# GLA levels on the columns of second block halves, and no meta columns after the last layer's mixing

## The chip, the cores and the metric

One core of a Trainium2 chip runs the whole program. The metric is the device time of one execution in microseconds. Before the change it is 2452.31 us (median of 3 runs, 2452.1 to 2452.59).

## The reference

One inference step of a decoder trunk with two layers, in float32. The columns (tokens) are 512 prompt tokens behind 16 learned meta tokens, and 8 samples of 4 tokens with a past of 512. Each layer is:

```
x += 0.5 * SwiGLU_1(RMSNorm(x))                      # 1024 -> 2 x 2816 -> 1024
h  = RMSNorm(x); columns of h @ W_in for three head groups
x += W_out [ FoX(h) | SSD(h) | GLA(h) ]              # forgetting attention, Mamba-2, gated linear attention
x += 0.5 * SwiGLU_2(RMSNorm(x))
```

The GLA group (4 heads, key 32, value 64) works in blocks of 128 tokens (16 for the meta tokens, 4 for a sample). With bc the running sum of the log gates of a block:

```
att = einsum('bthk,bshk,btshk->btsh', qc, kc, exp(bc_t - bc_s))     # s <= t
o   = att @ vc + (qc * exp(bc)) @ state
```

The result is y of the prompt without the meta tokens (`xp[:, N_META:]`), y of the samples, and the new keys, values, log forget values and states of both layers.

## The kernel before

x lies transposed in SBUF, 8 tiles of 128 rows by 560 columns: 32 of the samples, 16 meta columns, 512 of the prompt. Two groups of columns go through everything: A (columns 0 to 303: samples, meta, two blocks of the prompt; tiles 4, 0 and 1) and B (304 to 559: two blocks, tiles 2 and 3). Tile 4 holds the 48 columns of samples and meta tokens.

Every large product is made of three matmuls (`mm3`, line 427): weights and inputs are split into a high and a low part (`whi`, `wlo`, `hhi`, `hlo`, `hid`), and high x high, high x low and low x high are summed in PSUM. The weights come by DMA into `raw`, ScalarE casts the high part, VectorE (in the mixing stage each fifth time GpSimd) subtracts the low one.

A channel mixing (`ffn`) goes through 22 units of the hidden width, each with a gate and an up unit of weights: 24 matmuls on A, 24 on B. The down projection is done in three parts of 8, 8 and 6 units, in each for 8 tiles of rows. In the last part group A comes first, then B (`ffn_out`, the weights kept), so that A's norm runs beside B's matmuls. `norm` sums squares on ScalarE and GpSimd, turns the factor into rows on TensorE, and makes `hhi` and `hlo`.

The mixing stage (`mix`) names its pieces in `MIX_ORDER` (line 160); a scheduler of the framework then interleaves their instructions, engine by engine, so that the order on an engine is not that of the code. Each of the three head groups has a piece per tile: `fox_tile` (and `fox_meta` for the meta rows of tile 4, `fox_decode` for the samples), `ssd_tile`, `gla_tile`. They write into O; `split_o`, `mix_out` and `norm` follow.

`gla_tile` makes att by levels. For m = 64, 32, 16, 8, 4 a block of 2m columns has an early and a late half; key columns of the early half act on query columns of the late one. The first two levels of a tile of 128 columns are already made on the late halves alone (`z0`, `z1`, 256 columns for four heads). The others, m = 16, 8, 4 (in tile 4 the levels 8 and 4), are made on all columns: `zq` (lines 1221 and 1222; the third on GpSimd, being in `ON_POOL`) is the query times the gates for four heads, 512 columns, one fp32 matmul with the keys (line 1224) gives 128 x 512 values, and a masked copy (line 1225) puts those into `att` that the mask `lev` admits:

```
zq = self.g2(4 * n)
self.tt(zq..., z.unsqueeze(1).to_broadcast([128, 4, n]), qm, eng=self.e(f"gzq{i}"))
self.mm(pa[:n, :4 * n], kk, zq)
V.copy_predicated(out=att, mask=masks["lev"][:, i, :]..., data=pa[:n, :4 * n]...)
```

What is within a distance of three comes from `band` (line 1243). Tiles 4, 0, 1 of GLA come early in the stage, gla:2 and gla:3 late, beside SSD and FoX tiles and group A's output projection.

Of the kernel before, what the change touches and what calls it, by code (L numbers as in the profile page):

```python
# [25 lines left out]
F32R = mybir.dt.float32r  # L26
# [8 lines left out]
L = 2  # L35
D = 1024
# [50 lines left out]
def constants():  # L87
# [50 lines left out]
    for m in LEVS:  # L138
        s_, t_ = P[:, None], P[None, :]
        lev.append((s_ // (2 * m) == t_ // (2 * m)) & ((s_ // m) % 2 == 0) & ((t_ // m) % 2 == 1))  # L140
    put("lev", np.stack(lev[2:], 1))
    put("lev4", np.stack([v[:48, :48] & same for v in lev[3:]], 1))
    band = [k + d == t for d in (1, 2, 3)]
# [46 lines left out]
for _n, _w in (("gb", 128), ("fb", 4), ("db", 8), ("al", 8), ("sd", 8)):  # L190
# [37 lines left out]
class Trunk:  # L228
    def __init__(self, tc, a, es):
        self.tc, self.a = tc, a  # L230
        self.nc = nc = tc.nc
        self.V, self.S, self.G, self.T = nc.vector, nc.scalar, nc.gpsimd, nc.tensor
        pool = lambda n, b, **k: es.enter_context(tc.tile_pool(name=n, bufs=b, **k))
        self.pers = pool("pers", 1)
        self.wp = pool("wp", 2)
        self.hp = pool("hp", 1)
        self.tmp = pool("tmp", 1)
        self.psg = pool("psg", 2, space=PSUM)
        self.uid = 0
# [233 lines left out]
    def norm(self, g, gain, order=range(8)):  # L473
        c0, n = GRP[g]
        x = self.x
        acc = None
        for i, k in enumerate(order):
            sq = self.s1(304)
            self.act(sq[:, :n], x[:, k, c0:c0 + n], AF.Square)
            if i == 0:  # L480
                acc = sq
            else:
                self.tt(acc[:, :n], acc[:, :n], sq[:, :n], ALU.add, self.G if i < 7 else self.V)
        tiles = TILES[g]
# [8 lines left out]
        hi = self.t([128, 8, n], "hhi" + g, dt=F32R, pool=self.hp)  # L493
        lo = self.t([128, 8, n], "hlo" + g, dt=F32R, pool=self.hp)
        for k in range(8):
            h = self.s1(304)
            self.stt(h[:, :n], x[:, k, c0:c0 + n], gain[:, k:k + 1], y, ALU.mult, ALU.mult)
            self.act(hi[:, k, :], h[:, :n])
            eng = NORM_LO["mix" + g if self.lo_pool else g][k]
            self.tt(lo[:, k, :], h[:, :n], hi[:, k, :].bitcast(F32), ALU.subtract, self.G if eng == "G" else self.V)  # L500
        return hi, lo

    def ffn_in(self, l, i, fs, groups, H, hid, kept=None):

        for f in fs:
            pss = {}
            for gu in range(2) if kept is None or groups == "A" else (1, 0):
                w = self.kept_unit(kept, (f, gu), self.a["win"][l, i, f, gu], (f, gu) == (FIRST - 1, 1))
                for g in groups:
                    n = GRP[g][1]  # L510
                    ps = pss[gu, g] = self.ps(self.psg if g == "A" and (kept is None or f % 2 == 0) else self.psx)
                    hi, lo = H[g]
                    self.mm3(ps[:, :n], [(w[k], (hi[:, k, :], lo[:, k, :])) for k in range(8)])
            for g in groups:
                n = GRP[g][1]
                pg, pu = pss[0, g][:, :n], pss[1, g][:, :n]
# [64 lines left out]
    def hid_alloc(self, f, g):  # L581
        n = GRP[g][1]
        return tuple(self.t([128, n], "hid" + g, F32R, 16, self.hid) for _ in range(2))
# [250 lines left out]
    def fox_tile(self, g, i, c0):  # L834
# [6 lines left out]
        for hp in range(2):  # L841
# [32 lines left out]
            for k in range(i + 2):  # L874
                for h2, (et, emt) in enumerate(ets):
# [4 lines left out]
                    else:  # L880
                        self.mm(o, self.Vm[:, d], emt, start=False, stop=True)
        self.act(self.O[g][:, 0:2, c0:c0 + 128], po[:, 0:256].rearrange("p (a b) -> p a b", a=2))

# [117 lines left out]
    def ssd_tile(self, l, g, j, ti, c0, n):  # L1001
# [136 lines left out]
        for f in range(4):  # L1138
            self.tr(pt[:, f * n:(f + 1) * n], y[:, 128 * f:128 * f + 128])
        self.tt(self.O[g][:, 2:6, cs], pt[:, :4 * n].rearrange("p (f t) -> p f t", f=4), self.col["sn"].unsqueeze(2).to_broadcast([128, 4, n]))  # L1140


    def gla_tile(self, l, g, j, ti, c0, n):
# [31 lines left out]
        for h in range(4):  # L1175
            self.act(att[:, h, :], self.c("ident")[:n, :n], scale=dd[:, h:h + 1])
        masks = {m: self.c(m + ("4_r" if last else "_r")).rearrange("p (m t) -> p m t", t=n) for m in ("lev", "band")}

# [33 lines left out]
        for i in range(2 if last else 3):  # L1212
# [101 lines left out]
        for hp in range(2):  # L1314
            self.tr(pt[:, hp * n:(hp + 1) * n], on[:, 128 * hp:128 * hp + 128])
        for hp in range(2):
            self.stt(self.O[g][:, 6 + hp, cs], pt[:, hp * n:(hp + 1) * n], self.col["gn"], R[f"gg{hp}"][:, cs], ALU.mult, ALU.mult)

    def split_o(self, g):
        n = GRP[g][1]  # L1320
        hi = self.t([128, 8, n], "hhi" + g, F32R, pool=self.hp)
        lo = self.t([128, 8, n], "hlo" + g, F32R, pool=self.hp)
        for k in range(8):
# [5 lines left out]
    def mix_out(self, l, g, O):  # L1329
        c0, n = GRP[g]  # L1330
        hi, lo = O
# [9 lines left out]
    def mix(self, l, H):  # L1341
# [3 lines left out]
        nc.sync.dma_start(out=self.sconv.rearrange("p f b i -> p (f b i)"), in_=self.a["sconv"][l])  # L1345
        self.cvout = self.t([128, 6, 9, 3], "cvout")
        self.R = {"A": {}, "B": {}}
        self.O, S, N = {}, {}, {}
        run, live = {}, {}
        for g in GRP:  # L1350
            for j, (ti, c0, n) in enumerate(TILES[g]):
                run["gla", ti] = lambda a=(l, g, j, ti, c0, n): self.gla_tile(*a)
                run["ssd", ti] = lambda a=(l, g, j, ti, c0, n): self.ssd_tile(*a)
                run["fox", ti] = (lambda a=(g, ti, c0): self.fox_tile(*a)) if ti < 4 else self.fox_meta
            run["gla_in", g] = lambda g=g: self.gla_in(l, g, H)
# [105 lines left out]
def gather(r):  # L1461
# [24 lines left out]
```

## Time and profile before

| | |
|---|---|
| median of the runs | 2452.31 us |
| the profiled execution | 2455.32 us, its span 2453.5 us |
| TensorE | 2368.8 us busy (97%), granted clock 0.986 |
| VectorE | 1256.3 us (51%) |
| ScalarE | 869.7 us (35%) |
| GpSimd | 523.7 us (21%) |
| DMA engines | 230.57 MB, q1 29.9% |

The page cuts the span into 40 slices. In the channel mixings TensorE is busy in nine tenths of a slice or more and VectorE in three to four; in the two mixing stages (slices 9 to 14 and 29 to 34, counted from 1) VectorE is at seven to nine and the granted clock falls below full in some slices. A busy time is a sum over such different stages, so what a change is worth has to be read stage by stage.

### The profile page before, as it was taken

What the parts mean: (1) busy time and instruction counts of PE and PEld (TensorE: products, weight loads), DVE (VectorE), ACT (ScalarE), POOL (GpSimd) and SP (SyncE); (2) the same over time, 40 slices, a digit from 0 to 9 for tenths busy, and PEclk for the clock granted to TensorE, in tenths of its full rate; (3) what the DMA queues carried; (4) which work ended last, traced back from release to release, by engine and by line L of the source; (5) the groups of instructions that cost most, each with busy time, mean ns of one, the idle gap of its engine ahead of it and who ended that gap; (6) DMA issues with size and microseconds to landing.
All of it is one profiled execution on the core that took longest, in us unless ns stands there. A gap on an engine that the chain in (4) does not pass through costs nothing. (4 is left out here: it accounts for less than half of the span.)

```text
span 2453.5 us, 44862 instructions
## 1 busy us (share of the span) xinstructions
PE 2368.8 (97%) x17908; PEld 2254.9 (92%) x17908; DVE 1256.3 (51%) x2675; ACT 869.7 (35%) x1902; POOL 523.7 (21%) x688
## 2 busy tenths in 40 slices
PE   8999999999889999999999999999998999999999
PEld 8999999987777899999999999999776779999999
DVE  5434345388788533333443333343888985333333
ACT  4323223444354432322333232334343544323231
POOL 3202124233232310100221010131423324101010
PEclk9999999989899999999999999999899999999999
DMA  4222223344322322222222222232443222222222
GB/s 150 88 87 87 87 86 96 95 123 135 116 79 66 106 85 86 87 87 86 87 78 86 86 85 83 87 101 86 129 135 102 88 90 87 87 86 87 87 84 84
DMA packets 89683, 230.57 MB, mean 94 GB/s; under 512 B 12706, under 2 KB 38050, under 8 KB 89474
## 3 DMA queue, kind: packets, MB, share of 16 engines
q1 hardware_dynamic: 89042, 227.54, 29.9%
q8 instruction: 141, 2.31, 0.4%
q14 instruction: 68, 0.56, 0.1%
q10 hardware_dynamic: 432, 0.16, 0.0%
HBM read 219.73 MB, written 7.92 MB: 93 GB/s over the span
## 5 line engine op out<-in xcount | busy, mean ns | idle before, releaser
L272 DVE TENSOR_TENSOR wlo<-raw,whi 128x512 fp32r<-128x512 f32 (+1 forms) x649 | 464.1, 718 | 404.5 <-ACT whi L278 395.1
L278 ACT ACTIVATE whi<-raw 128x512 fp32r<-128x512 f32 (+1 forms) x680 | 427.0, 631 | 646.0 <-PE ps L265 589.3
L265 PE MATMUL ps<-hhiA,wlo 128*128 128x304 f32 x1664 | 507.5, 305 | 0.0
L265 PE MATMUL ps<-hhiA,whi 128*128 128x304 f32 x1664 | 506.8, 305 | 0.0
L265 PE MATMUL ps<-hloA,whi 128*128 128x304 f32 x1664 | 505.6, 304 | 0.0
L265 PE MATMUL ps<-hhiB,wlo 128*128 128x256 f32 x1664 | 471.2, 283 | 4.4 <-POOL wlo L272 3.0
L265 PE MATMUL ps<-hhiB,whi 128*128 128x256 f32 x1664 | 469.6, 283 | 2.0 <-ACT s L278 0.9
L265 PE MATMUL ps<-hloB,whi 128*128 128x256 f32 x1664 | 469.5, 282 | 0.0
L265 PEld LDWEIGHTS ps<-hhiB,whi 128*128 128x128 f32 x1664 | 315.0, 189 | 6.1 <-issue 1.9
L265 PEld LDWEIGHTS ps<-hhiB,wlo 128*128 128x128 f32 x1664 | 315.2, 190 | 5.6 <-POOL wlo L272 3.2
L265 PEld LDWEIGHTS ps<-hhiA,wlo 128*128 128x128 f32 x1664 | 314.8, 189 | 3.9 <-issue 3.0
L265 PEld LDWEIGHTS ps<-hloA,whi 128*128 128x128 f32 x1664 | 315.3, 189 | 2.8 <-issue 2.0
L265 PEld LDWEIGHTS ps<-hhiA,whi 128*128 128x128 f32 x1664 | 314.7, 189 | 2.6 <-issue 1.4
L265 PEld LDWEIGHTS ps<-hloB,whi 128*128 128x128 f32 x1664 | 314.5, 189 | 2.3 <-issue 1.5
L272 POOL TENSOR_TENSOR hidA<-s,hidA 128x304 fp32r<-128x304 f32 x88 | 76.0, 864 | 849.2 <-ACT hidA L278 849.1
L265 PE MATMUL ps<-hidA,whi 128*128 128x304 f32 x1072 | 226.2, 302 | 0.0
L275 DVE SCALAR_TENSOR_TENSOR x<-ps,x 128x304 f32<-128x304 f32 (+1 forms) x192 | 86.0, 449 | 232.3 <-PE ps L265 230.7
L265 PE MATMUL ps<-hidB,whi 128*128 128x256 f32 x1072 | 193.9, 281 | 0.0
L265 PEld LDWEIGHTS ps<-hidA,whi 128*128 128x128 f32 x1072 | 174.4, 188 | 0.0
L265 PEld LDWEIGHTS ps<-hidB,whi 128*128 128x128 f32 x1072 | 166.2, 189 | 0.0
L272 DVE TENSOR_TENSOR s<-s,ps 128x256 f32<-128x256 f32 (+3 forms) x194 | 90.4, 467 | 145.7 <-PE ps L265 137.6
L265 PE MATMUL ps<-hidA,wlo 128*128 128x304 f32 x536 | 162.1, 302 | 0.0
(334 smaller groups left out, 3579.9 us busy)
## 6 DMA issues: line engine op xcount, KB each, us to landing
raw<-win SPq DMA_DIRECT2D x176, 512.0 KB, 3.5
raw<-wout SPq DMA_DIRECT2D x64, 512.0 KB, 3.5
raw<-wfm SPq DMA_DIRECT2D x48, 512.0 KB, 3.5
raw<-wmo SPq DMA_DIRECT2D x32, 512.0 KB, 3.6
raw<-wout SPq DMA_DIRECT2D x32, 384.0 KB, 3.5
pg<-kpage SPq DMA_DIRECT2D x64, 130.0 KB, 2.2
pg<-vpage SPq DMA_DIRECT2D x64, 128.0 KB, 2.3
raw<-wtm SPq DMA_DIRECT2D x8, 544.0 KB
```

Source lines behind the costliest of these rows:

```text
L265: return self.T.matmul(out, lhsT, rhs, start=start, stop=stop, **k)
L272: return (eng or self.V).tensor_tensor(out=out, in0=a, in1=b, op=op)
L275: return self.V.scalar_tensor_tensor(out=out, in0=a, scalar=s, in1=b, op0=op0, op1=op1)
L278: return self.S.activation(out, in_, f, **k)
```

## The change

In `gla_tile` the levels m = 16, 8, 4 are made on the late halves alone: `zq` has 2n columns in place of 4n, the matmul streams 2n, and the masked copy reads 2n and writes the late halves of `att`. The masks keep only those columns. In the last layer, from the output projection on, group A has 288 columns: at the head of its mixing stage the 32 sample columns of x are copied 16 columns up, over the meta columns, and `GRP_END`, `TILES_END` take the place of `GRP`, `TILES`; the tiles write into O without the meta columns, `fox_meta` is not called there, and the samples are read from y at 16 to 47.

```diff
-    put("lev", np.stack(lev[2:], 1))
-    put("lev4", np.stack([v[:48, :48] & same for v in lev[3:]], 1))
+    odd = lambda v, m: v[:, (np.arange(v.shape[1]) // m) % 2 == 1]
+    put("lev", np.stack([odd(v, m) for v, m in zip(lev[2:], LEVS[2:])], 1))
+    put("lev4", np.stack([odd(v[:48, :48] & same, m) for v, m in zip(lev[3:], LEVS[3:])], 1))
...
+GRP_END = {"A": (16, 288), "B": GRP["B"]}
+TILES_END = {"A": [(4, 0, 32), (0, 32, 128), (1, 160, 128)], "B": TILES["B"]}
...
     def norm(self, g, gain, order=range(8)):
-        c0, n = GRP[g]
+        c0, n = self.grp[g]
...
-        self.act(self.O[g][:, 0:2, c0:c0 + 128], po[:, 0:256].rearrange("p (a b) -> p a b", a=2))
+        self.act(self.O[g][:, 0:2, self.ocols(g, c0, 128)[0]], po[:, 0:256].rearrange("p (a b) -> p a b", a=2))
...
-            zq = self.g2(4 * n)
-            self.tt(zq.rearrange("p (h t) -> p h t", h=4), z.unsqueeze(1).to_broadcast([128, 4, n]), qm, eng=self.e(f"gzq{i}"))
+            m = LEVS[(3 if last else 2) + i]
+            half = lambda a: a.rearrange("p (b i m) -> p b i m", i=2, m=m)[:, :, 1, :]
+            zq = self.g2(2 * n)
+            zv = zq.rearrange("p (h b m) -> p h b m", h=4, m=m)
+            qv = qm.rearrange("p h (b i m) -> p h b i m", i=2, m=m)[:, :, :, 1, :]
+            self.tt(zv, half(z).unsqueeze(1).to_broadcast(list(qv.shape)), qv, eng=self.e(f"gzq{i}"))
             pa = self.ps(self.psL)
-            self.mm(pa[:n, :4 * n], kk, zq)
-            V.copy_predicated(out=att, mask=masks["lev"][:, i, :].unsqueeze(1).to_broadcast([n, 4, n]),
-                              data=pa[:n, :4 * n].rearrange("p (h t) -> p h t", h=4))
+            self.mm(pa[:n, :2 * n], kk, zq)
+            pv = pa[:n, :2 * n].rearrange("p (h b m) -> p h b m", h=4, m=m)
+            V.copy_predicated(out=att.rearrange("p h (b i m) -> p h b i m", i=2, m=m)[:, :, :, 1, :],
+                              mask=masks["lev"][:, i, :].rearrange("p (b m) -> p b m", m=m).unsqueeze(1).to_broadcast(list(pv.shape)), data=pv)
...
+    def ocols(self, g, c0, n):
+        if self.grp is GRP or g == "B":
+            return slice(c0, c0 + n), n
+        return (slice(0, 32), 32) if c0 == 0 else (slice(c0 - 16, c0 - 16 + n), n)
...
+        if l == L - 1:
+            self.grp, self.tiles = GRP_END, TILES_END
+            for o in (32, 16):
+                self.G.tensor_copy(self.x[:, :, o:o + 16], self.x[:, :, o - 16:o])
...
-                run["fox", ti] = (lambda a=(g, ti, c0): self.fox_tile(*a)) if ti < 4 else self.fox_meta
+                run["fox", ti] = (lambda a=(g, ti, c0): self.fox_tile(*a)) if ti < 4 else self.fox_meta if l < L - 1 else lambda: None
```

`ffn_in`, `ffn_out`, `split_o`, `mix_out` and `hid_alloc` read `self.grp` in the same way as `norm`.

The program is ordered by the scheduler, so the instructions move as well. TensorE in tile gla:3 of the last layer, before (names: `g` by `g` are the GLA levels, `hhiA`, `hloA` the inputs of the output projection, `kaug`, `qaug` a FoX score, `gpr` the band):

```order
L265 MATMUL ps_22678<-g_3968_22679,g_3966_22676 128x256
L265 MATMUL ps_22678<-g_3969_22682,g_3966_22676 128x256
L265 LDWEIGHTS c_identb_978
L265 MATMUL ps_22899<-c_cmask_r_494,c_identb_978 128x128
L265 MATMUL ps_22691<-g_3970_22689,g_3966_22676 128x512
L265 MATMUL ps_22698<-g_3973_22696,g_3972_22694 128x512
L265 MATMUL ps_22651<-c_hsel_650,gpr_22706 128x4
L265 MATMUL ps_23096<-hhiA_22299,whi_23088 128x304
L265 MATMUL ps_23096<-hloA_22300,whi_23088 128x304
L265 MATMUL ps_22703<-g_3975_22701,g_3972_22694 128x512
```

and after the change:

```order
L271 MATMUL ps_22651<-g_3959_22652,g_3957_22649 128x256
L271 MATMUL ps_22651<-g_3960_22655,g_3957_22649 128x256
L271 MATMUL ps_22664<-g_3961_22662,g_3957_22649 128x256
L271 LDWEIGHTS c_identb_978
L271 MATMUL ps_22872<-c_cmask_r_494,c_identb_978 128x128
L271 MATMUL ps_23069<-hhiA_22272,whi_23061 128x288
L271 MATMUL ps_23069<-hloA_22273,whi_23061 128x288
L271 MATMUL ps_22624<-c_hsel_650,gpr_22679 128x4
L271 MATMUL ps_22671<-g_3964_22669,g_3963_22667 128x256
L271 MATMUL ps_23069<-hhiA_22272,wlo_23062 128x288
L271 MATMUL ps_23069<-hhiA_22272,whi_23061 128x288
L271 MATMUL ps_22676<-g_3966_22674,g_3963_22667 128x256
```

The last three level matmuls have 256 columns for 512, and two matmuls of the output projection (288 columns) and one of the band now stand between the first and the second of them.

VectorE at the same place, before (`gqm` the query by heads, `gk` the key, `att` is the `g` that the masked copies write):

```order
L272 TENSOR_TENSOR g_3970_22689<-g_3962_22665,gqm_22674 128x512
L272 TENSOR_TENSOR g_3972_22694<-g_3964_22672,gk_21687 128x256
L272 TENSOR_TENSOR g_3973_22696<-g_3964_22672,gqm_22674 128x512
L272 TENSOR_TENSOR gpr_22706<-gdq_22708,gk_21687 128x127
L272 TENSOR_TENSOR gqk_22729<-g_3964_22672,gk_21687 128x128
L1225 COPY_PREDICATED g_3958_22655<-c_lev_r_666,ps_22691 128x512
L272 TENSOR_TENSOR gdq_22708<-gdq_22708,g_3964_22672 128x127
L1225 COPY_PREDICATED g_3958_22655<-c_lev_r_666,ps_22698 128x512
L272 TENSOR_TENSOR gpr_22706<-gdq_22708,gk_21687 128x126
L272 TENSOR_TENSOR x_70<-x_70,ps_22872 128x304
L1225 COPY_PREDICATED g_3958_22655<-c_lev_r_666,ps_22703 128x512
L272 TENSOR_TENSOR gdq_22708<-gdq_22708,g_3964_22672 128x126
```

and after:

```order
L278 TENSOR_TENSOR g_3961_22662<-g_3953_22638,gqm_22647 128x256
L278 TENSOR_TENSOR g_3963_22667<-g_3955_22645,gk_21660 128x256
L278 TENSOR_TENSOR g_3964_22669<-g_3955_22645,gqm_22647 128x256
L278 TENSOR_TENSOR gpr_22679<-gdq_22681,gk_21660 128x127
L278 TENSOR_TENSOR gqk_22702<-g_3955_22645,gk_21660 128x128
L278 TENSOR_TENSOR gdq_22681<-gdq_22681,g_3955_22645 128x127
L1238 COPY_PREDICATED g_3949_22628<-c_lev_r_666,ps_22664 128x16x16
L278 TENSOR_TENSOR gpr_22679<-gdq_22681,gk_21660 128x126
L1238 COPY_PREDICATED g_3949_22628<-c_lev_r_666,ps_22671 128x32x8
L278 TENSOR_TENSOR gdq_22681<-gdq_22681,g_3955_22645 128x126
L1238 COPY_PREDICATED g_3949_22628<-c_lev_r_666,ps_22676 128x64x4
L278 TENSOR_TENSOR x_70<-x_70,ps_22845 128x288
```

The two products have 256 columns; the masked copies write 16x16, 32x8 and 64x4; the update of x by the output projection, which stood in front of the third masked copy, stands behind it.

GpSimd at the end of the last layer's first channel mixing, in the changed program (`hloA` the low part of group A's norm, `s` the sum of squares of group B):

```order
L278 TENSOR_TENSOR hloA_18682<-s_3084_18703,hhiA_18681 128x304
L1371 COPY x_70<-x_70 128x8x16
L278 TENSOR_TENSOR hloA_18682<-s_3085_18707,hhiA_18681 128x304
L1371 COPY x_70<-x_70 128x8x16
L278 TENSOR_TENSOR s_3095_18875<-s_3095_18875,s_3096_18877 128x256
L278 TENSOR_TENSOR s_3095_18875<-s_3095_18875,s_3097_18880 128x256
```

The two copies of x are new; they stand before and behind the last step of group A's norm.

## Rows read from the trace of the kernel before

**Rows 1.** stretches: from:to, length, engines' busy time (instructions), clock, DMA share, GB/s.

```profile
520.00:660.00 140.00, 130.98 (x958) 101.14 (x956) 111.81 (x302) 53.34 (x143) 47.59 (x88) 0.91 0.43 130
1735.00:1880.00 145.00, 134.15 (x1001) 103.71 (x1002) 116.55 (x314) 55.20 (x149) 50.37 (x91) 0.95 0.43 129
1880.00:2048.00 168.00, 148.22 (x1015) 126.53 (x1013) 143.50 (x306) 86.32 (x222) 60.99 (x67) 0.98 0.28 90
2048.00:2450.00 402.00, 401.71 (x3118) 401.74 (x3119) 143.79 (x258) 109.00 (x209) 40.30 (x47) 1.00 0.27 83
1634.00:1650.00 16.00, 15.86 (x133) 15.66 (x133) 8.52 (x19) 6.50 (x16) 10.54 (x16) 1.00 0.12 35
```

**Rows 2.** the chain that ended last, its longest piece; start, length, what.

```profile
2048.29 402.18 PE ps L265 x3120
```

**Rows 3.** timeline of TensorE in the last channel mixing: start, length of the record.

```profile
2345.02 0.30 PE L265 MATMUL ps<-hhiA,whi 128*128 128x304 f32 x1
...
2348.36 0.27 PE L265 MATMUL ps<-hhiB,whi 128*128 128x256 f32 x1
...
2351.20 0.30 PE L265 MATMUL ps<-hhiA,whi 128*128 128x304 f32 x1
```

**Rows 4.** groups by form, by line and by tile: busy us, mean ns; or min/median/max.

```profile
L272 DVE TENSOR_TENSOR g<-g,gqm 128x512 f32<-128x512 f32 x16 | 17.3, 1079 | 1.3 <-PE ps L265 1.3
L1225 DVE COPY_PREDICATED g<-c_lev_r,ps x28: 352/724/742, 525.1 to 1973.2; 128x512 f32<-128x512 uint8 x24, 48x192 f32<-48x192 uint8 x4
L272 POOL TENSOR_TENSOR g<-g,gqm x8: 1279/1387/1759, 551.8 to 1968.6; 128x512 f32<-128x512 f32 x8
```

**Rows 5.** timeline of TensorE in the first layer's last GLA tile.

```profile
755.29 0.59 PE L265 MATMUL ps<-g,g 128*128 128x512 f32 x1
755.72 0.59 PE L265 MATMUL ps<-Sgl,gzc 128*128 128x256 f32 x2
756.15 0.28 PE L265 MATMUL ps<-c_hsel,gpr 128*128 128x4 f32 x2
```

**Rows 6.** timelines of VectorE and, last row, GpSimd in gla:2 and gla:3, last layer.

```profile
1925.33 0.68 DVE L272 TENSOR_TENSOR g<-g,gqm 128x512 f32<-128x512 f32 x1
1968.49 0.41 DVE L272 TENSOR_TENSOR g<-g,gk 128x256 f32<-128x256 f32 x1
1968.83 1.75 DVE L272 TENSOR_TENSOR g<-g,gqm 128x512 f32<-128x512 f32 x1
1968.65 1.38 POOL L272 TENSOR_TENSOR g<-g,gqm 128x512 f32<-128x512 f32 x1 [1.36 <-DVE g L272]
```

**Rows 7.** chain by line in 1735 to 1880 and 1880 to 2060 us, and pieces.

```profile
by line: PE ps L265 59.2%; issue 10.6%; PE ps L269 4.1%; DVE s L272 3.6%; POOL s L272 2.9%; DVE qaug L275 2.6%; DVE kaug L275 2.4%; DMA pg<-vpage 2.2%; POOL gst L310 1.7%; POOL gqk L272 1.5%; DVE wlo L272 1.3%; POOL gqm L272 1.0%; DVE g L27
by line: PE ps L265 46.4%; issue 10.2%; PE ps L269 5.1%; DVE s L275 4.5%; POOL hloA L272 3.9%; DVE g L272 3.8%; ACT s L278 3.3%; DVE wlo L272 2.7%; DVE s L272 2.6%; POOL s L272 2.3%; DMA raw<-win 1.9%; POOL sss L310 1.4%; ACT g L278 1.3%; A
1766.86 17.00 PE ps L265 x123
1966.50 4.08 DVE g L272 x7
1970.72 2.47 PE ps L265 x8
1973.21 0.74 DVE g L1225
```

**Rows 8.** timeline of VectorE, `fox_meta` of the last layer.

```profile
1826.02 0.71 DVE L908 COPY O<-ps 64x16 f32<-64x16 f32 x4
```

**Rows 9.** line 725 (ns min/median/max) and the timeline of GpSimd.

```profile
L725 POOL COPY s<-sconv x12: 199/210/552, 475.7 to 1803.7; 128x24 f32<-128x24 f32 x12
1974.90 0.41 POOL L272 TENSOR_TENSOR gpr<-gdq,gk 128x125 f32<-128x125 f32 x1 [0.29 <-DVE gdq L272]
```

**Rows 10.** timeline of TensorE in the first layer's mixing stage.

```profile
530.98 0.46 PE L265 MATMUL ps<-hhiA,whi 128*128 128x304 f32 x1
531.23 0.46 PE L265 MATMUL ps<-hloA,whi 128*128 128x304 f32 x1
```

More of the change, by code (lines that the diff above doesn't have):

```diff
@@ L241, in __init__ @@
         self.nlo, self.lo_pool = 0, 0
+        self.grp, self.tiles = GRP, TILES
     def t(self, shape, tag, dt=F32, bufs=1, pool=None):
@@ L483, in norm @@
                 self.tt(acc[:, :n], acc[:, :n], sq[:, :n], ALU.add, self.G if i < 7 else self.V)
-        tiles = TILES[g]
+        tiles = self.tiles[g]
         pool = self.psn[g]
@@ L492, in norm @@
             self.tr(y[:, o:o + 128], r[:, j:j + 1].to_broadcast([128, 128]))
-        hi = self.t([128, 8, n], "hhi" + g, dt=F32R, pool=self.hp)
-        lo = self.t([128, 8, n], "hlo" + g, dt=F32R, pool=self.hp)
+        hi = self.t([128, 8, GRP[g][1]], "hhi" + g, dt=F32R, pool=self.hp)[:, :, :n]
+        lo = self.t([128, 8, GRP[g][1]], "hlo" + g, dt=F32R, pool=self.hp)[:, :, :n]
         for k in range(8):
@@ L509, in ffn_in @@
                 for g in groups:
-                    n = GRP[g][1]
+                    n = self.grp[g][1]
                     ps = pss[gu, g] = self.ps(self.psg if g == "A" and (kept is None or f % 2 == 0) else self.psx)
@@ L514, in ffn_in @@
             for g in groups:
-                n = GRP[g][1]
+                n = self.grp[g][1]
                 pg, pu = pss[0, g][:, :n], pss[1, g][:, :n]
@@ L536, in ffn_out @@
             for g in groups:
-                c0, n = GRP[g]
+                c0, n = self.grp[g]
                 ps = self.ps(self.psg if g == "A" and kept is None else self.psx)
@@ L581, in hid_alloc @@
     def hid_alloc(self, f, g):
-        n = GRP[g][1]
+        n = self.grp[g][1]
         return tuple(self.t([128, n], "hid" + g, F32R, 16, self.hid) for _ in range(2))
@@ L1139, in ssd_tile @@
             self.tr(pt[:, f * n:(f + 1) * n], y[:, 128 * f:128 * f + 128])
-        self.tt(self.O[g][:, 2:6, cs], pt[:, :4 * n].rearrange("p (f t) -> p f t", f=4), self.col["sn"].unsqueeze(2).to_broadcast([128, 4, n]))
+        os, m = self.ocols(g, c0, n)
+        self.tt(self.O[g][:, 2:6, os], pt[:, :4 * n].rearrange("p (f t) -> p f t", f=4)[:, :, :m], self.col["sn"].unsqueeze(2).to_broadcast([128, 4, m]))
     def gla_tile(self, l, g, j, ti, c0, n):
@@ L1176, in gla_tile @@
             self.act(att[:, h, :], self.c("ident")[:n, :n], scale=dd[:, h:h + 1])
-        masks = {m: self.c(m + ("4_r" if last else "_r")).rearrange("p (m t) -> p m t", t=n) for m in ("lev", "band")}
+        masks = {m: self.c(m + ("4_r" if last else "_r")).rearrange("p (m t) -> p m t", t=n if m == "band" else n // 2) for m in ("lev", "band")}
         zd = self.t([128, 128], "gzc")
@@ L1315, in gla_tile @@
             self.tr(pt[:, hp * n:(hp + 1) * n], on[:, 128 * hp:128 * hp + 128])
+        os, m = self.ocols(g, c0, n)
         for hp in range(2):
-            self.stt(self.O[g][:, 6 + hp, cs], pt[:, hp * n:(hp + 1) * n], self.col["gn"], R[f"gg{hp}"][:, cs], ALU.mult, ALU.mult)
+            self.stt(self.O[g][:, 6 + hp, os], pt[:, hp * n:hp * n + m], self.col["gn"], R[f"gg{hp}"][:, c0:c0 + m], ALU.mult, ALU.mult)
+    def ocols(self, g, c0, n):
+        if self.grp is GRP or g == "B":
+            return slice(c0, c0 + n), n
+        return (slice(0, 32), 32) if c0 == 0 else (slice(c0 - 16, c0 - 16 + n), n)
     def split_o(self, g):
-        n = GRP[g][1]
-        hi = self.t([128, 8, n], "hhi" + g, F32R, pool=self.hp)
-        lo = self.t([128, 8, n], "hlo" + g, F32R, pool=self.hp)
+        n = self.grp[g][1]
+        hi = self.t([128, 8, GRP[g][1]], "hhi" + g, F32R, pool=self.hp)[:, :, :n]
+        lo = self.t([128, 8, GRP[g][1]], "hlo" + g, F32R, pool=self.hp)[:, :, :n]
         for k in range(8):
@@ L1329, in mix_out @@
     def mix_out(self, l, g, O):
-        c0, n = GRP[g]
+        c0, n = self.grp[g]
         hi, lo = O
@@ L1361, in mix @@
             run["norm", g] = lambda g=g: N.update({g: self.norm(g, self.col["g2"])})
-            run["O", g] = lambda g=g: self.O.update({g: self.t([128, 8, 304], "O")[:, :, :GRP[g][1]]})
+            run["O", g] = lambda g=g: self.O.update({g: self.t([128, 8, 304], "O")[:, :, :self.grp[g][1]]})
         run["decode", "A"] = lambda: self.fox_decode(l)
@@ L1476, in gather @@
     smp = lambda a: a[:, sample].reshape((L, 8, 4) + a.shape[2:])
-    out = (y[48:][None], y[sample].reshape(8, 4, D), fk[:, prompt][:, None], fv[:, prompt][:, None], lf[:, prompt][:, None],
+    out = (y[48:][None], y[16:48].reshape(8, 4, D), fk[:, prompt][:, None], fv[:, prompt][:, None], lf[:, prompt][:, None],
            sp, cv[:, 8:9], gp, smp(fk), smp(fv), smp(lf), ss, cv[:, 0:8], gs)
```

## The prediction

> **What bounds the kernel now.** I read the stretches first, then the chain, then single rows. The reader is to see two different regimes. From 2048 us to the end (the last layer's second channel mixing) TensorE never stops: 401.7 of 402 us busy at a granted clock of 1.00, VectorE at 36% [rows 1], and the chain that ended last is one unbroken piece of 3120 matmuls there [rows 2]. What shortens a matmul in that stretch shortens the kernel, one for one. In the mixing stages, where the GLA tiles are, it is different: in 1735 to 1880 us TensorE is busy 134 and VectorE 117 of 145 us, in 1880 to 2048 us 148 and 144 of 168 us [rows 1], and the chain changes hands all the time: TensorE holds 63% of it in the first of these stretches and 52% in the second (taken to 2060 us), VectorE, GpSimd, ScalarE and waits the rest [rows 7]. There a saving counts only where its engine stands on the chain at that moment. Layer 0 has the same stage (520 to 660 us reads like 1735 to 1880 us).
>
> **The meta columns.** From the last output projection on, group A has 288 columns for 304. Matmuls concerned: 8x24 in the output projection, 22x2x24 in the gate and up projections, 8x22x3 in the down projection, together 192 + 1056 + 528 = 1776. Their price per column is read from one unit of 24 on each group: A (304 columns) starts at 2345.02 and B at 2348.36, so 3.34 us or 139.2 ns each; B (256 columns) lasts until 2351.20, so 2.84 us or 118.3 ns each [rows 3]. 20.9 ns for 48 columns is 0.43 ns a column; 16 columns are 6.8 to 7.0 ns (6.7 ns if it is 16 cycles at 2.4 GHz). 288 lies between two sizes that both run gapless, so no floor is met: 1776 x 6.8 = 12.1 us, of which 10.8 us lie in the stretch where nothing but TensorE counts, the 1.3 us of the output projection in the mixing stage. Bounds: 11.8 and 12.4 us.
>
> The Trainium skill speaks against this size: "TensorE: Matmul & The Clock Gate", section "Back-to-back issue gap", gives for a stream of weight loads and matmuls about 81 ns at 128 columns and 131 ns at 512. Straight between these, an estimate from that page, 16 columns would be 2.1 ns and the whole edit 3.7 us in place of 12.1. The rows differ from it (139.2 ns at 304, 20.9 ns more than at 256), and I go by the rows.
>
> Also gone is the attention of the meta rows in the last layer (`fox_meta`). Its VectorE part stands on the chain; its four copies into O alone take 0.71 us [rows 8], and with the scaling before them it is near 1.0 us. I take 1.0; bounds 0 (what is queued behind waits for something else) and 3 us (its TensorE pieces and its softmax count too).
>
> Added: two GpSimd copies of 8x16 columns of x at the head of the last mixing stage. They stand before and behind the last GpSimd step of group A's norm. Neither size is in the trace: a copy of 24 elements takes 0.21 us, a two-input operation on 125 columns 0.41 us [rows 9], so 0.2 to 0.4 us each, and I take 0.4, the nearer size. TensorE is meanwhile in group B's down projection (15.9 of 16 us busy from 1634 to 1650 us [rows 1]): cost nothing; 0.8 us if that cover were gone. The smaller masks and their casts lie in the first channel mixing: nothing.
>
> **The GLA levels.** Of eight tiles of 128 columns, three levels each (24) go from 512 to 256 columns; of two small tiles, two levels each from 192 to 96.
> TensorE: the program lists a level as one matmul, the trace shows two records. A record of 512 columns takes 0.43 us (755.29 to 755.72), two of 256 columns also 0.43 us (755.72 to 756.15) [rows 5]. So 24 x 2 x 0.215 = 10.3 us, and 0.6 us for the small tiles: 10.9 us of TensorE.
> VectorE, the products: 16 of the 24 are its own, mean 1079 ns [rows 4]. That mean hides two cases. Alone, 512 columns take 0.68 us; behind a GpSimd product that runs in the same moment they take 1.75 us (1968.83, GpSimd 1968.65 for 1.38) [rows 6]. Both halve, since 256 columns take 0.41 us [rows 6] and GpSimd's own third product (8 of them, near 1.4 us [rows 4]) halves too. I take 0.55 for 1.08: 16 x 0.53 = 8.5 us.
> VectorE, the masked copies: 724 ns at 512 columns and 352 ns at 192 [rows 4], 1.16 ns a column, so 0.43 us at 256: 24 x 0.295 = 7.1 us. With 0.6 us for the small tiles VectorE loses 16.2 us in all.
>
> The new operations read and write runs of 16, 8 and 4 columns. No row shows this on a large tile. The nearest: a GpSimd copy of eight runs of three takes 0.21 us [rows 9]; even if all of that were run cost it would be 26 ns a run, and the 112 runs of a tile, once in the product and once in the copy, would add up to 5.8 us a tile. I take zero, since 0.21 us is what such small operations take anyway; the far end is kept for a rival. The Trainium skill has such a price: "GPSIMD Engine Reference", section "Performance pitfalls for Q7 kernels", puts some 102 cycles on each small read command. If every run of four were one, a rough estimate from that page is 5 us for one GpSimd product; the row of 0.21 us for eight runs does not look like it, but eight runs are few.
>
> What of this is on the path, tile by tile in the last layer: gla:0 and gla:1 stand where TensorE holds the chain (a piece of 17 us among others [rows 7]): 6 x 0.43 = 2.6 us. gla:2 stands where VectorE is full: two products less 0.27 each, three copies less 0.30 each, 1.4 us. gla:3 is on the chain itself (4.08 us of VectorE, 2.47 us of TensorE, 0.74 us for the last masked copy [rows 7]): its products give 0.27 + 0.85, one matmul 0.43, the last copy 0.30, 1.85 us. The small tile 0.3. Sum 6.1 us a layer, 12.2 us for two. I count 10 of it: as soon as a tile is through sooner, the next thing that it waits for (statistics on GpSimd, pages of values) ends last. Bounds: 0 (the other waits decide everywhere) and 27 us (both engines' savings count in full).
>
> The edit also moves instructions: the order is made by a scheduler, and from the first GLA tile on in either layer it comes out differently on all engines. In gla:3 TensorE now has two matmuls of the output projection between the first level and the second, which stood together. That can give or take a few microseconds a layer; I take zero.
>
> **Sum.** 12.1 + 10 + 1.0 = 23.1 us. The profiled execution took 2455.32 us (span 2453.5 and 1.8 around it), so 2432.2; that execution is 3.0 us over the median of the runs, 2452.31, so 2429 us in their terms.
>
> **Rivals.**
> (a) The GLA savings go into other waits and only the columns count: 2452.3 - 12.1 = 2440 us (2436 to 2444 with the scheduler's give and take). For it: waits and other engines hold over a third of the chain in the mixing stages. Against it: gla:0 and gla:1 lie in pieces of TensorE's.
> (b) VectorE, not TensorE, is the real limit from 1880 us on (85% busy there [rows 1]), and both savings add up: 12.1 + 10.9 + 16.2 + 1 = 40 us at most, 2412; halfway 2418. Against it: where TensorE is full, VectorE's time is free.
> (c) Short runs cost: 5.8 us a tile are 46 us over eight, 33 of them on VectorE (GpSimd has the products of the third level, 64 runs a tile). They eat VectorE's 16 us and 17 more; with those on the chain in full and TensorE's share left, 2452.3 - 12.1 - 1 - 5 + 17 = 2451, no change. For it: no row has 64 runs. Against it: the size of the row of eight runs. (The page on GpSimd named above would lead here.)
> (d) Slower: TensorE waits more, with its matmuls shorter, and is granted its lower level. At 1.2 GHz the 304-column matmuls of the mixing stage start 0.25 us apart (530.98, 531.23) [rows 10] against 0.139 us [rows 3], 0.11 us lost on each. To end 5 us above before it must eat 28 us, about 255 such matmuls or 64 us of the two mixing stages at the lower level beyond what is there. For it: the clock is 0.91 and 0.95 in the stages where GLA starts [rows 1]. Price 2457 or more.
> (e) 288 columns are nearly as dear as 304, the fall from 139.2 to 118.3 ns coming mostly below 288, which no row excludes wholly: at 2 ns a matmul 1776 of them give 3.6 us, and 2452.3 - 3.6 - 11 = 2438. Against it: both ends stand near their columns divided by 2.4 GHz, 126.7 and 106.7 ns, with the same 12 ns on top. (The page on TensorE named above would give about this.)
>
> **How the numbers follow.** The sum: 0.62, its own range 2421 to 2437. (a) 0.18, (b) 0.12, (c) 0.03, (d) 0.02, (e) 0.03. Leaving out less than two in ten: 2415 to 2441. A difference under 0.2%, about 5 us, is what a measurement of this kernel can't tell from none. Faster by more: 0.62 + 0.18 + 0.12 + 0.03, less a little for a scheduler's bad order on top of (a): 0.94. Within: (c) and that little, 0.04. Slower: (d), 0.02.
>
> **What would show it.** In the profile after: matmuls of 288 columns that start 132 ns apart, and an unbroken last piece of the chain 10 to 11 us shorter than 402. The level records at 256 columns near 0.21 us apart, masked copies of 16x16, 32x8 and 64x4 all near 0.43 us; if the three differ, (c) has something. The stage from the last norm before mixing to that last piece about 7 us shorter in the last layer (5 GLA, 1 meta, 1.3 columns) and about 5 us in layer 0. I am wrong if the last piece does not shrink, or if either mixing stage is longer than before.

## The result and the profile after

The changed kernel takes 2424.62 us, median of four runs (2420.72 to 2429.23), against 2452.45 us before: a ratio of 0.988, 95% interval 0.985 to 0.991. The forecast was 2429 us. A second series of the same kernel on another chip (`r_after`, below) gave 2424.04 us and 0.9881, 0.986 to 0.990. By these intervals the saving is 23 to 36 us in the first series and 24 to 34 in the second; the 23 of the forecast lie at the edge of the one and just below the other. What comes on top is not where the columns are. The profiled execution took 2423.02 us.

The page of the kernel after, its first lines; the kernel before had 2453.5 us, PE 2368.8, DVE 1256.3, POOL 523.7:

```profile
span 2421.2 us, 44803 instructions
PE 2342.0 (97%) x17889; PEld 2243.2 (93%) x17889; DVE 1242.4 (51%) x2667; ACT 866.0 (36%) x1900; POOL 522.5 (22%) x690
```

For the stages, both traces are cut at one point that each of them has, the GpSimd power in group B's norm. Five stretches follow: the first mixing stage, two channel mixings, the second mixing stage, the last channel mixing. Columns as in [rows 1]; here the kernel before:

```profile
433.90:825.30 391.40, 359.78 (x2593) 305.58 (x2592) 295.88 (x731) 179.84 (x455) 123.86 (x183) 0.96 0.35 107
825.30:1240.30 415.00, 411.82 (x3178) 410.64 (x3177) 163.07 (x292) 128.47 (x251) 61.31 (x70) 1.00 0.28 87
1240.30:1652.10 411.80, 411.14 (x3185) 410.16 (x3184) 155.01 (x283) 124.36 (x243) 59.57 (x75) 1.00 0.27 83
1652.10:2042.10 390.00, 356.44 (x2591) 301.14 (x2590) 297.37 (x731) 178.77 (x454) 124.77 (x182) 0.98 0.35 107
2042.10:2453.50 411.40, 407.37 (x3150) 406.92 (x3149) 148.48 (x268) 112.74 (x217) 44.12 (x51) 1.00 0.27 84
```

And the same five of the kernel after:

```profile
433.30:818.10 384.80, 353.11 (x2592) 305.15 (x2590) 291.33 (x731) 178.62 (x455) 125.18 (x182) 0.96 0.35 108
818.10:1233.30 415.20, 411.51 (x3179) 410.60 (x3179) 163.05 (x292) 128.45 (x251) 61.16 (x70) 1.00 0.28 88
1233.30:1646.40 413.10, 412.45 (x3185) 411.50 (x3184) 155.15 (x283) 124.06 (x243) 59.89 (x76) 1.00 0.27 82
1646.40:2020.30 373.90, 346.17 (x2573) 299.92 (x2571) 288.67 (x722) 178.04 (x452) 122.97 (x181) 0.97 0.36 111
2020.30:2421.20 400.90, 397.05 (x3150) 396.61 (x3149) 148.22 (x269) 111.65 (x217) 43.33 (x51) 1.00 0.28 87
```

The reader is to see three things. The last channel mixing is 10.5 us shorter, and TensorE's busy time there falls by as much (10.3). The channel mixings between, which the change does not touch, stay within 1.3 us. The mixing stages give 6.6 and 16.1 us where about 5 and 7 were expected.

The columns first. TensorE's timeline of one unit on each group, kernel after, beside [rows 3]:

```profile
2345.54 0.29 PE L271 MATMUL ps<-hhiA,whi 128*128 128x288 f32 x1
...
2348.72 0.27 PE L271 MATMUL ps<-hhiB,whi 128*128 128x256 f32 x1
...
2351.56 0.29 PE L271 MATMUL ps<-hhiA,whi 128*128 128x288 f32 x1
```

24 matmuls of 288 columns take 3.18 us, 132.5 ns each, for 139.2 before; 256 columns are still 118.3. The chain's last piece, beside [rows 2]:

```profile
2021.95 396.23 PE ps L271 x3145
```

It is only 5.95 us shorter, and holds 25 matmuls more: it starts 1.65 us behind the norm's power (2020.3) and not 6.2 (2048.29 against 2042.1). A piece of the chain begins where the last wait ends, so two pieces are not the same stretch; the stage cut at the norm is.

The level operations by form, beside [rows 4] (the 24 products on VectorE are 16 of the levels m = 16 and 8, and 8 that had 256 columns before):

```profile
L278 DVE TENSOR_TENSOR g<-g,gqm 128x256 f32<-128x256 f32 x24 | 14.2, 592 | 0.0
L1238 DVE COPY_PREDICATED g<-c_lev_r,ps 128x256 f32<-128x256 uint8 x24 | 10.3, 430 | 2.0 <-PE ps L271 1.5
L278 POOL TENSOR_TENSOR g<-g,gqm 128x256 f32<-128x256 f32 x8 | 6.5, 816 | 3.8 <-DVE g L278 3.8
```

VectorE's timeline in gla:3 of the last layer, kernel after, beside [rows 6, 7]:

```profile
1948.39 0.29 DVE L278 TENSOR_TENSOR gzc<-g,gq 128x128 f32<-128x128 f32 x1 [0.83 <-ACT g L284]
...
1950.81 0.94 DVE L278 TENSOR_TENSOR g<-g,gqm 128x256 f32<-128x256 f32 x1
...
1952.28 0.42 DVE L1238 COPY_PREDICATED g<-c_lev_r,ps 128x256 f32<-128x256 uint8 x1
...
1952.97 0.43 DVE L1238 COPY_PREDICATED g<-c_lev_r,ps 128x256 f32<-128x256 uint8 x1
...
1953.66 0.44 DVE L1238 COPY_PREDICATED g<-c_lev_r,ps 128x256 f32<-128x256 uint8 x1
```

The same row `gzc` opens the tile before:

```profile
1966.15 0.29 DVE L272 TENSOR_TENSOR gzc<-g,gq 128x128 f32<-128x128 f32 x1 [0.83 <-ACT g L278]
```

From there to the end of the last level copy it is 5.71 us, and was 7.80 (to 1973.95 [rows 7]): 2.1 us where 1.85 were forecast. The product beside GpSimd fell from 1.75 to 0.94 us. The three copies, in runs of 16, 8 and 4 columns, cost the same.

The two copies of x are in GpSimd's line 1371, inside the norm; the trace shows no engine that waited for them:

```profile
L1371 POOL COPY x<-x x2: 283/410/536, 1634.8 to 1635.8; 128x128 f32<-128x128 f32 x2
```

### The profile page after: what moved, and what is told of

The parts are those of the page before. It is cut to its first block, busy times and chain, and to the rows that moved or that the text cites. A ratio compares the mean times of both kernels' runs of the same rounds, so it can differ in the third digit from the quotient of the medians.

```text
span 2421.2 us, 44803 instructions
## 1 busy us (share of the span) xinstructions
PE 2342.0 (97%) x17889; PEld 2243.2 (93%) x17889; DVE 1242.4 (51%) x2667; ACT 866.0 (36%) x1900; POOL 522.5 (22%) x690
## 5 line engine op out<-in xcount | busy, mean ns | idle before, releaser
L271 PE MATMUL ps<-hhiA,whi 128*128 128x304 f32 (+1 forms) x1664 | 505.8, 304 | 0.0
L271 PE MATMUL ps<-hloA,whi 128*128 128x304 f32 (+1 forms) x1664 | 504.1, 303 | 0.0
L271 PE MATMUL ps<-hhiA,wlo 128*128 128x304 f32 (+1 forms) x1664 | 503.5, 303 | 0.0
L278 POOL TENSOR_TENSOR hidA<-s,hidA 128x304 fp32r<-128x304 f32 (+1 forms) x88 | 74.9, 851 | 839.2 <-ACT hidA L284 839.2
L271 PE MATMUL ps<-hidA,whi 128*128 128x304 f32 (+1 forms) x1072 | 223.4, 300 | 0.0
L281 DVE SCALAR_TENSOR_TENSOR x<-ps,x 128x304 f32<-128x304 f32 (+2 forms) x192 | 85.5, 446 | 229.5 <-PE ps L271 227.8
L278 DVE TENSOR_TENSOR s<-s,ps 128x256 f32<-128x256 f32 (+4 forms) x194 | 89.8, 464 | 142.1 <-PE ps L271 133.9
L271 PE MATMUL ps<-hidA,wlo 128*128 128x304 f32 (+1 forms) x536 | 161.0, 300 | 0.0
```

The costliest lines, as they stand in the source:

```text
L271: return self.T.matmul(out, lhsT, rhs, start=start, stop=stop, **k)
L278: return (eng or self.V).tensor_tensor(out=out, in0=a, in1=b, op=op)
L281: return self.V.scalar_tensor_tensor(out=out, in0=a, scalar=s, in1=b, op0=op0, op1=op1)
```

## The experiments

All results in one table; the stages are those of each kernel's profiled execution, idle is stage length less TensorE's busy time, over both mixing stages.

| kernel | us, median (range) | ratio to before, 95% | mixing 1st + 2nd | TensorE idle |
|---|---|---|---|---|
| before | 2452.45 | | 391.4 + 390.0 = 781.4 | 65.2 |
| after | 2424.62 (2420.72–2429.23) | 0.988 (0.985–0.991) | 384.8 + 373.9 = 758.7 | 59.4 |
| r_after | 2424.04 (2421.92–2427.95) | 0.9881 (0.986–0.990) | 382.6 + 376.7 = 759.3 | 63.1 |
| e1_halves | 2439.36 (2435.63–2445.30) | 0.9937 (0.992–0.995) | 381.9 + 378.8 = 760.7 | 62.1 |
| e2_meta | 2441.16 (2437.12–2443.31) | 0.9936 (0.992–0.995) | 391.1 + 385.6 = 776.7 | 63.1 |
| e3_foxmeta | 2426.69 (2424.29–2432.86) | 0.9885 (0.987–0.990) | 380.9 + 380.7 = 761.6 | 67.6 |
| e4_twice | 2422.95 (2421.48–2425.05) | 0.9865 (0.985–0.988) | 381.9 + 377.4 = 759.3 | 57.5 |
| e5_dve_twice | 2454.54 (2446.81–2457.59) | 0.9999 (0.999–1.001) | 396.1 + 389.2 = 785.3 | 75.1 |
| e6_late_copies | 2422.73 (2420.60–2423.68) | 0.9870 (0.985–0.989) | 383.3 + 376.4 = 759.7 | 64.5 |
| e7_four_times | 2451.24 (2445.28–2457.37) | 0.9990 (0.998–1.000) | 395.6 + 387.7 = 783.3 | 58.7 |
| e8_product_twice | 2439.62 (2438.11–2452.14) | 0.9949 (0.993–0.997) | 389.0 + 386.0 = 775.0 | 69.8 |
| e9_copy_twice | 2426.90 (2425.80–2430.60) | 0.9889 (0.987–0.991) | 381.0 + 381.5 = 762.5 | 64.5 |
| e10_pool_to_dve | 2426.33 (2424.23–2433.08) | 0.9887 (0.987–0.990) | 384.3 + 380.4 = 764.7 | 65.2 |
| e11_full_product | 2432.92 (2431.70–2433.80) | 0.9907 (0.989–0.992) | 387.4 + 379.6 = 767.0 | 59.3 |

A ratio is to runs of the kernel before that were taken beside it; beside e1 to e11 and r_after their medians are 2455.0 to 2455.8 us, and the 2452.45 belong to the first series. One mixing stage of one profile is good to some 4 us: the first one, the same code in after, r_after, e3 and e6, reads 384.8, 382.6, 380.9 and 383.3. The idle time is no better: after and r_after are one kernel and have 59.4 and 63.1 us.

**Each half alone.** e1 keeps the meta columns, e2 the full levels; the edits against the changed kernel, in words:

```
-  os, m, self.grp, fox_meta of the last layer, copies of x   (e1: as before)
-  zq, matmul and masked copy on second halves                (e2: as before)
```

> Only the GLA levels are cut to their second halves; the meta columns stay to the end. Theory 1 (the prediction's sum: levels about 5 us a layer, columns 12.1, fox_meta 1): 10 us less than before, about 2442, with the first mixing stage 6 to 7 us shorter and the second no more than that, and the last channel mixing unchanged (its last chain piece again 402 us over 3120 instructions). Rival A (the second mixing stage is 16 us shorter because of the GLA itself, which the two stages weigh differently): about 2434 to 2436, with the second mixing stage 12 to 15 us shorter. Rival B (the GLA's gain needs the meta drop's new order): within 3 us of the first stage's gain alone, about 2446.

> Only the meta columns are dropped; the GLA levels run at full width. Theory 1: 12.1 us of columns and 1 us of fox_meta, about 2439, with 10.6 us of it in the last channel mixing and 2 to 3 in the second mixing stage. Rival A as in the run before (the surplus belongs to the GLA): the same 2439. Rival C (taking fox_meta out of the second mixing stage is worth what the statistics markers show, 4 to 5 us, and more through the order that follows): 2431 to 2435, with the second mixing stage 6 to 10 us shorter and the first unchanged.

e1 saves 15.4 us by its ratio (12 to 19), e2 15.7 (12 to 19); together 31, and the whole change 29: they add. The second mixing stage and the last channel mixing of e2:

```profile
1652.80:2038.40 385.60, 355.74 (x2573) 302.12 (x2571) 294.53 (x722) 177.94 (x452) 122.59 (x181) 0.96 0.34 108
2038.40:2439.40 401.00, 397.07 (x3151) 396.64 (x3149) 148.19 (x269) 112.04 (x217) 43.41 (x51) 1.00 0.27 87
```

The meta drop's 14.8 us there are 10.4 in the last channel mixing and 4.4 in the second mixing stage, of which the output projection's columns explain 1.3. So the GLA is worth 14 to 17 us, more than forecast, as rival A has it; but e1's two stages gain 9.5 and 11.2 us, so the second is not the 12 to 15 of A, nor the first the 6 to 7 of Theory 1. That the last channel mixing stays as it was holds: the last piece of e1's chain is 402.16 us long, with 3120 instructions. Rival B's 2446 and rival C's 2431 to 2435 both fail.

**The price of fox_meta.** The edit, in words:

```
-  self.fox_meta if l < L - 1 else lambda: None
+  self.fox_meta          (last layer: into a scratch tile)
```

> The changed kernel, but the last layer's fox_meta is still run, its result put into a tile that nobody reads. Theory 1: fox_meta costs 1 us on the path, so about 1 us over the changed kernel, 2425 to 2426. Rival C: its whole work stands in the way, 4 to 6 us more, about 2429 to 2431, and all of it in the second mixing stage between the statistics of gla:1 and those of ssd:4.

Its ratio is 0.0004 above r_after's (1 us), its median 2.7 us, its second mixing stage 4.0 us. So fox_meta is worth 1 to 4 us; Theory 1's 1 us and the lower end of rival C's 4 to 6 are not told apart, 2 to 3 is the middle. Where in the stage it lies was not looked at.

**TensorE's part of the levels.** e4 streams the columns twice, e7 four times (in words):

```
-  self.mm(pa[:n, :2 * n], kk, zq)
+  self.mm(pa[:n, :4 * n] in 2 x 2n, kk, zq repeated twice)     # e7: this, twice
```

> The changed kernel, but each level matmul streams its 256 columns twice (512 columns, as many as before the change), so the products and masked copies stay short and TensorE's half of the saving is given back. Theory 1 (of the 10 us, TensorE's 10.9 us of columns stand on the path nearly whole wherever TensorE holds the chain, 5.4 of 6.1 us a layer in the tile by tile count): 7 to 10 us more than the changed kernel, 2432 to 2435. Rival D (VectorE's products and copies are what the level chain waits for): under 4 us more, at most 2428.

> The changed kernel, but each level matmul streams its 256 columns four times (1024 columns, twice what it had before the change): 32.7 us more TensorE work in all, three times what streaming twice adds. Theory D (TensorE has room beside the levels' other work): at most 6 us over the changed kernel. Theory 1 (columns on the path; streaming twice looked free by chance): 20 us or more over it. Theory E (streaming twice does cost 3 us or so, and a higher granted clock in the two mixing stages pays for it): 6 to 12 us more, with the clock above that of the changed kernel.

Giving TensorE back all of its 10.9 us costs nothing: e4 is not slower than r_after, and the two mixing stages add up to 759.3 us in both. The expectation puts 5.4 of the 6.1 us a layer on TensorE; the prediction itself has 3.0 there (2.6 in gla:0 and gla:1, 0.43 in gla:3), 5 to 6 us for two layers, and that too did not come. r_after's two stages:

```profile
433.10:815.70 382.60, 349.48 (x2593) 302.76 (x2592) 291.83 (x731) 179.09 (x455) 126.04 (x183) 0.97 0.35 109
1642.50:2019.20 376.70, 346.71 (x2572) 300.45 (x2571) 289.12 (x722) 178.09 (x452) 123.19 (x182) 0.97 0.35 110
```

Those of e4:

```profile
433.00:814.90 381.90, 352.37 (x2591) 301.94 (x2590) 292.40 (x731) 179.22 (x455) 120.22 (x183) 0.98 0.34 109
1643.20:2020.60 377.40, 349.41 (x2573) 299.50 (x2571) 290.04 (x722) 178.56 (x452) 122.07 (x182) 0.97 0.35 110
```

Against r_after TensorE is busy 5.6 us longer and idle 5.6 us less (against after, 2.5 and 1.9); half of the 10.9 us or more does not appear at all, with the granted clock at 0.98 and 0.97 (0.97 and 0.97). Four times, 32.7 us of columns, costs 27 us: the step from twice to four times, 21.8 us of columns, shows in full and more (27 to 31 us), the step from once to twice not at all. So Theory D holds for the change's own size and falls beyond it; the 20 us that Theory 1 wants come only there. Theory E fails as it stands: 27 us are not 6 to 12, and e7's granted clock, 0.983 to 0.988, is not above r_after's 0.985 to 0.989. But e4's is, at 0.988 to 0.991. Over all runs on record a run is about 1.5 us shorter for each 0.001 of clock that it has above other runs of its kernel; by this estimate e4 would be some 3 us slower than r_after at the same clock. Why its clock is higher is not shown. The two ran on different chips, but there the kernel before has much the same, 0.985 and 0.986 on average.

**VectorE's and GpSimd's part.** e5 does products and copies twice, e8 the products, e9 the copies.

```
+  for _ in range(2):                       # e5, e8
       self.tt(zv, half(z)..., qv, eng=self.e(f"gzq{i}"))
+  for _ in range(2):                       # e5, e9
       V.copy_predicated(out=att... second halves, mask, data=pv)
```

> The changed kernel, but each level's product and each masked copy is done twice over the same half columns, so VectorE and GpSimd have about the work of before the change and TensorE keeps its shorter matmuls. Theory D (the levels are bound by their products and copies; the run with twice the columns took no longer): nearly the whole gain of the halves is lost, 12 to 16 us over the changed kernel, 2436 to 2440. Theory 1 (TensorE's columns carried the gain): at most 5 us over it, under 2430.

> The changed kernel, but only the levels' products are done twice (20 more on VectorE, 8 more on GpSimd), the masked copies once. Theory D, as the run with both twice left it (29 us of added work cost 30 us, so each of these us is on the path): the products' 15 to 17 us, 2438 to 2442. Rival G (products run ahead of their matmuls, and only the copies end a level): at most 6 us over the changed kernel, under 2430.

> The changed kernel, but only the masked copies are done twice (28 more on VectorE, 12 us), the products once. Theory D: 11 to 14 us over the changed kernel, 2435 to 2438, and with the run beside it about the 30 us of both. Rival G (only the copies end a level): 20 us or more over it.

e5 gives back the whole gain and the columns' too: 29 to 31 us for 20 more products and 28 more copies on VectorE and 8 products on GpSimd, about twice what Theory D said. e8 costs 15.6 us (Theory D's 15 to 17), e9 2 to 3 us (neither's; far under Theory D's 11). Rival G fails in both. The costs do not add: 18 us singly, 29 to 31 together. The two mixing stages of e5:

```profile
433.70:829.80 396.10, 357.43 (x2592) 307.21 (x2590) 299.78 (x755) 179.27 (x455) 126.43 (x187) 0.95 0.33 105
1658.20:2047.40 389.20, 352.80 (x2573) 303.71 (x2571) 295.94 (x746) 178.25 (x452) 125.61 (x185) 0.96 0.34 107
```

Against r_after they are 26.0 us longer: 12.0 us are TensorE idle (75.1 for 63.1), and 14.0 us are TensorE busy longer with the same 5165 matmuls, at a granted clock of 0.95 and 0.96 for 0.97 and 0.97. So the added work shows twice, as gaps and in slower matmuls. e8 has the same split, 6.7 and 9.0 us. Stages of e8, then of e9:

```profile
433.60:822.60 389.00, 355.29 (x2593) 308.98 (x2592) 292.00 (x741) 178.56 (x455) 124.57 (x187) 0.96 0.34 107
1649.30:2035.30 386.00, 349.89 (x2571) 301.57 (x2570) 293.00 (x732) 176.33 (x452) 126.79 (x185) 0.96 0.35 108
433.10:814.10 381.00, 350.71 (x2589) 302.35 (x2588) 295.61 (x746) 180.92 (x457) 118.48 (x183) 0.97 0.36 111
1642.20:2023.70 381.50, 347.26 (x2573) 299.93 (x2572) 295.12 (x736) 178.43 (x452) 121.37 (x182) 0.97 0.35 109
```

The gaps do not stand in front of the level matmuls. These rows have the matmuls of all levels, r_after and then e5; the number behind the second bar is TensorE's idle time just before them, 2.3 and 1.4 us in all:

```profile
L271 PE MATMUL ps<-g,g 128*128 128x256 f32 x80 | 23.5, 400 | 2.3 <-DVE g L278 1.8 <-ACT gdb L284 0.5
L271 PE MATMUL ps<-g,g 128*128 128x256 f32 x80 | 23.9, 400 | 1.4 <-DVE g L278 0.8 <-DVE g L1240 0.6
```

What grew is waits for other work of VectorE: for line 866, the scaling of FoX's softmax, TensorE waited 1.2 us in r_after (2 times) and 9.0 in e5 (6 times). Here the two who-waited rows of that line:

```profile
  PE ps L275: 1.2, 2
  PE ps L275: 9.0, 6
```

But VectorE's busy time is not the price either: in the two mixing stages it is 14.8 us above r_after's in e5, 4.1 in e8 and 9.8 in e9, and e9 is the cheap one. e5 and e8 also double the eight products on GpSimd, e9 does not. No run lengthens the products of one of the two engines alone, so which of them counts stays open.

**Only the products undone.**

```
-  zq = self.g2(2 * n)     # products of second halves
+  zq = self.g2(4 * n)     # all columns; the matmul reads the second halves of zq
```

> The changed kernel with one part undone: the levels' products go over all 512 columns again (48 columns a head in the short tiles), while the matmul streams, and the copy moves, only the second halves. Theory P (the products carry the gain of the halves, as doing them twice cost 15 us, the copies twice 2 us and the columns twice nothing): 11 to 16 us over the changed kernel, 2435 to 2440, with the two mixing stages together longer by as much. Rival Q (doing a step twice costs by its extra instructions and not by its length; the gain needs all three parts): at most 6 us over it, under 2430.

6.4 us by the ratios, 8.9 by the medians, 7.7 in the mixing stages: between Theory P and rival Q. Its products on VectorE and GpSimd (256 columns in the rows of the kernel after, above):

```profile
L278 DVE TENSOR_TENSOR g<-g,gqm 128x512 f32<-128x512 f32 x16 | 13.3, 830 | 2.4 <-PE ps L271 2.4
...
L278 POOL TENSOR_TENSOR g<-g,gqm 128x512 f32<-128x512 f32 x8 | 11.9, 1491 | 7.1 <-DVE g L278 7.1
```

VectorE's mean is 830 ns here and was 1079 before the change [rows 4], so e11 does not bring back all of the products' old time. Its two mixing stages:

```profile
432.80:820.20 387.40, 357.77 (x2591) 307.69 (x2589) 294.37 (x731) 179.64 (x455) 125.84 (x182) 0.95 0.34 108
1648.70:2028.30 379.60, 349.96 (x2572) 302.82 (x2570) 289.00 (x722) 178.85 (x452) 127.33 (x182) 0.96 0.35 110
```

Against r_after TensorE is idle 3.8 us less (59.3 for 63.1) and busy 11.5 us longer at a lower clock: all of e11's cost in this profile is slower matmuls.

In time as measured the products carry the largest single part, about half of the 14 to 17 us. Undoing all three parts costs those 14 to 17 us (e2 against after); given back alone, the columns cost nothing, and doubled, the copies 2 to 3 us. The rest comes only with several parts together.

**Order and engine.** e6 puts the copies of x before the first output projection; e10 takes `gzq2` off the list of GpSimd's operations.

```
-  G.tensor_copy(x ... shifted by 16)  at the head of the mixing stage   # e6: before out:A
-  ON_POOL = [..., "gqk", "gzq2", "sr1", ...]                            # e10
+  ON_POOL = [..., "gqk", "sr1", ...]
```

> The changed kernel, but the two copies that shift x by 16 columns are put just before the first output projection of the last layer; no work is added or taken. Theory 1: the copies are hidden, within 2 us of the changed kernel. Rival F (where the copies stand shapes the order of the second mixing stage, and the surplus of 9 us there is from that): 4 us or more slower, with the second mixing stage longer by as much.

> The changed kernel, but the 8 products of the third level go to VectorE, where the others take 0.42 to 0.6 us, instead of GpSimd with 0.84. Theory D (the level chain itself is the limit, whatever engine a step of it is on): 2 to 3.5 us faster than the changed kernel, about 2421. Rival H (VectorE's total work is the limit, not the chain): 3 to 5 us slower, 2427 to 2429.

e6 is as fast as the changed kernel (1.3 us less, inside both ranges): rival F falls for this place. e10 is not faster; 1.5 to 2.3 us the other way is within what the runs can tell, so neither theory is shown. No version here beats the changed kernel by more than the runs can tell.

## Why the prediction came out as it did

- **The columns**: right. 132.5 ns for a matmul of 288 columns (132 forecast), 10.5 us in the last channel mixing (10.8 forecast). Rival (e) is dead. The estimate from the Trainium skill ("TensorE: Matmul & The Clock Gate", section "Back-to-back issue gap") made the whole edit worth 3.7 us; the trace differs, 10.4 us in the last channel mixing alone in e2. The sign that was named for it, a last piece of the chain 10 to 11 us shorter, did not come (5.95 us), because the piece begins at another place.
- **fox_meta**: 1 to 4 us measured, 1.0 taken, 3 the upper bound: mis-sized low, if at all.
- **The GLA levels**: 10 us counted, 14 to 17 measured. The term is too small, and a step behind it failed: "TensorE where TensorE holds the chain" gave half of the tile count, 3.0 of 6.1 us a layer, to the columns (all of gla:0 and gla:1, and 0.43 us in gla:3). Giving the columns back cost nothing in time (e4); the products alone give back about half of the gain (e11), products and copies doubled all of it and more (e5). That the tile count of 12.2 us was near is luck in part: 2.6 us in gla:0 and gla:1 were put on an engine that had room, and e5 shows a way that the count does not have, VectorE's and GpSimd's work in the levels holding up other pieces, FoX's among them. A likely reason why the chain names TensorE there, not shown, is that it works through other matmuls while the level waits.
- **Rival (b)** had the right side, VectorE's, where the runs leave open how much is GpSimd's, and a wrong sum: TensorE's savings and VectorE's do not add. Halfway from the forecast to its 2412 is 2420 to 2421, not the 2418 that it gives; the measured 2424.6 lies between that and the forecast.
- **Rival (a)** needed savings lost in other waits; e1's 15 us exclude it. **Rival (c)**: copies in runs of 16, 8 and 4 columns all take 0.42 to 0.44 us, and GpSimd's products in runs of 4 take 0.82 us for 1.42; no price. **Rival (d)**, a lower clock with shorter matmuls, did not come: the granted clock of the mixing stages is 0.96 and 0.97 after, 0.96 and 0.98 before. The other way round something like it is seen: the kernels with longer products have a lower clock (e5, e8, e11).
- **The scheduler's order**, taken as zero: e6 says nothing is to be had by moving the copies of x; other orders were not tried. The 16.1 us of the second mixing stage in the first profile are 13.3 in r_after, so part of the surplus there was one execution's.
- **Open**: what the clock has to do with it. Every kernel's runs follow it (r_after: 2421.92 us at 0.989, 2427.95 at 0.985), and the kernels with longer products have less of it in every run or nearly (e5 0.977 to 0.983, e11 0.982 to 0.984, r_after 0.985 to 0.989). By the estimate of 1.5 us for 0.001, e11 would cost 2 us at r_after's clock, e9 5, e8 9 and e5 19, and the whole change would still save 28 to 29. At an equal clock, then, the products stand out less: doubled 9 us against 5 for the copies and 3 for the columns, and undone only 2. That they are half of the gain holds only if the lower clock is their doing. Whether gap or clock comes first was not tried.

## What to carry to other kernels

Where a chain passes between two engines, the engine that the chain names need not be the one whose work is too long: give each part of a saving back alone, and see which one the time follows. Parts of one saving need not add, in either direction, so undo them singly and together. Where TensorE never stopped, in the last channel mixing, a shorter matmul was worth its columns, one for one.

## What the runs showed of the hardware

- A matmul stream costs 139.2, 132.5 and 118.3 ns at 304, 288 and 256 columns: columns at 2.4 GHz and 12 ns more, at a granted clock of 1.00 and on this one line.
- A masked copy of 256 columns takes 0.42 to 0.44 us in runs of 16, 8 or 4.
- The same 5165 matmuls of the mixing stages were busy 696.2 us in r_after (granted clock 0.97 and 0.97) and 710.2 in e5 (0.95 and 0.96), where TensorE waited 12 us more between them.
- In the mixing stages TensorE took 10.9 us more of fp32 columns without a longer time (e4, at a clock of 0.988 to 0.991 for 0.985 to 0.989); the next 21.8 us cost 27 to 31 (e7).
